# The last stretch of a seven-product block multiplication, in three parts of 256, 128 and 128 tokens in place of two of 256

## Chip, cores and metric

The kernel runs on one core of a Trainium2 chip. Its time is the device time of one execution in microseconds (us). A core has five engines that work beside each other, each through a queue of its own: TensorE (PE in the profile, its weight loads PEld), VectorE (DVE), ScalarE (ACT), GpSimd (POOL) and SyncE (SP), which issues DMAs; ScalarE and GpSimd issue some DMAs too. Engines wait for one another through semaphores.

## What is computed

A trunk of two layers over 1024 tokens of 1024 channels, each a token mixer and a SwiGLU feed-forward part, with RMS norms and scale and gate values made from a conditioning vector, and one RMS norm at the end. Cut to what matters here:

```python
def rms_norm(x, g):
    y = x * rsqrt(mean(x * x, axis=-1, keepdims=True) + EPS)
    return y * g

def swiglu_ffn(h, w_gate, w_up, w_down):
    return (silu(h @ w_gate) * (h @ w_up)) @ w_down

for i in range(DEPTH):
    ...
    h = modulate(rms_norm(x, norm_ffn_g[i]), sh_f, sc_f)
    y = swiglu_ffn(h, ffn_w_gate[i], ffn_w_up[i], ffn_w_down[i])
    x = x + (1.0 + g_f) * y
return rms_norm(x, final_g)
```

The change is in the last product with `w_down` of the second layer and in the final norm of half of the tokens.

## The kernel before

Channels lie on the 128 partitions, so `x` is eight tiles of 128 channels by tokens (k = 0 to 7), and tokens are in two chunks of 512, A (0) and B (1). The tiles of a chunk lie in pairs in SBUF, and two tiles of a pair go out in one DMA.

A weight or an activation is kept as two parts of rounded 32-bit numbers (`F32R`): `hi`, rounded, and `lo`, the rest. A product of the two is three matmuls into one bank of PSUM (`products`, L496): high by high, high by low, low by high. Each matmul loads 128x128 weights and streams the tokens past them. Sums for the norms and the spreading of a row over partitions are matmuls of plain 32-bit numbers, which the trace shows as two records each.

The product with `w_down` in the second layer is done by Strassen's scheme, with seven block products in place of eight (`Seven`, L1489), each over up to six groups of feature blocks (q) and with sums of 512 tokens in four PSUM banks `dn`, one for each output tile. When a product is complete, `update` (L1008) adds it, times the gate, to `x`. The last of the seven, `p3`, is split: its first three groups of q run as the others do and are added to the lower four tiles of chunk B, and the remaining ones (`LAST`, three groups) run in `ending` (L1570). That is the last stretch of the kernel.

In `ending`, `emit` (L1614) goes over the parts of `ENDS` (L37): first tokens 0 to 255 of chunk B, then 256 to 511. For each part and each of the four output tiles d there are 18 matmuls (three groups of two feature blocks, three matmuls each), then on VectorE `x += gate * dn` (a SCALAR_TENSOR_TENSOR `x<-dn,gains,x`), on ScalarE the square (`t<-x`), and on VectorE its sum into `acc`. The squares of the upper four tiles were summed ahead (`upper`, L1602). In the last part the squares of the last two d are not summed on VectorE, but go to the norm's matmuls directly (`STRAIGHT`).

The norm of a part is a generator, `normed` (L1579), that is advanced step by step:

1. It is made behind the part's last d and waits.
2. `var`: one matmul for every 128 tokens and every term of the sum, with the squares as weights and a column of ones as the moving operand, which leaves the mean squares as columns; then the reciprocal root, eight small VectorE instructions on `var` and `col`. ScalarE then multiplies the part of all eight tiles by the final gain (`x<-x,vecs`), at a lower priority.
3. `rstd`: one matmul for every 128 tokens spreads the root over the partitions; ScalarE copies it to SBUF (`ny`); in all parts but the last GpSimd multiplies six of the eight tiles by `ny`.
4. VectorE multiplies the others by `rstd`. In the last part VectorE has six tiles and GpSimd two. Behind each pair of tiles the output's DMA is issued: by ScalarE for k = 1 and 5, by SyncE for k = 3 and 7 (`scaled`, L1572).

While the second part's products run, the first part's norm is advanced at d = 1 (step 2) and d = 3 (step 3). The rest is issued behind the last product. Chunk A's final norm (`final`, L1644) runs in the same stretch, its `rstd` between the products of the first part, and its scalings on VectorE and GpSimd.

TensorE's order is the order in which the code issues it. The other engines' orders are made by a scheduler from the program's order, priorities and its own estimates. Each engine then runs its queue strictly in that order: a DMA that ScalarE issues stands in ScalarE's queue, and what is behind it waits until its data is ready.

Of the kernel before, what the change touches and what calls it, by code (L numbers as in the profile page):

```python
# [33 lines left out]
CHUNKS = ((0, 512), (512, 512))  # L34
CENTRED = (0, 2, 3, 1, 5, 6, 4, 7)

ENDS = ((0, 256), (256, 256))  # L37
NP = NF // 2
GROUP = 4
ROUND = 4  # L40
# [91 lines left out]
def trunk(ctx, tc, xT, c, vec, ada, adan, w1f, w1, wdg, w2, wgu, wdn, wds, wpl, out):  # L132
# [91 lines left out]
    def pace(ahead=AHEAD):  # L224

        for t in [t for t in tasks if t.urgent or getattr(t, "free", False)]:
            while step(t, "V"):
                pass
        moved = True
        while moved and tasks:  # L230
            moved = False
            for e in "VG":
                if clock[e] < clock["PE"] + ahead:
                    moved = any(step(t, e) for t in list(tasks)) or moved
# [62 lines left out]
    def bank(name):  # L297
        return ps.tile([P, 512], F32, tag="mm", name=nm(name))
# [15 lines left out]
    def temp(n, name="t", bufs=0):  # L314
        t = tmp.tile([P, TMPW], F32, tag=name if bufs else "t", name=nm(name), bufs=bufs or 4)
        return t[:, :n]
# [53 lines left out]
    def V(name, j, n=1):  # L370
        b = _COLS[name] + j
        return vecs[:, b : b + n]
# [123 lines left out]
    def products(out, wt, k, act, first, last, o=0, n=None, more=False):  # L496

        wk = slice(k * P, (k + 1) * P)
        for i, (wp, a) in enumerate(((0, 0), (0, 1), (1, 0))):
            cols = act[a][:, o : o + n] if n else act[a]  # L500
            matmul(out, wt[:, wp, wk], cols, start=first and i == 0, stop=last and i == 2, more=more)
# [114 lines left out]
    def xsub(ch, k, o, n):  # L616
        return x[ch.i][k][:, o : o + n]
# [5 lines left out]
    def now(gen):  # L623

        while True:
            try:
                next(gen)
            except StopIteration as e:
                return e.value
# [940 lines left out]
    def ending(ch, l):  # L1570

        def scaled(k, o, n, rstd, eng):  # L1572
            xs = xsub(ch, k, o, n)
            eng.tensor_tensor(xs, xs, rstd, op=MUL)
            if k % 2:
                (nc.scalar if k % 4 == 1 else nc.sync).dma_start(
                    out[:, k - 1 : k + 1, ch.t0 + o : ch.t0 + o + n], xp[ch.i][k // 2][:, :, o : o + n])

        def normed(o, n, acc, last):  # L1579
            steps = mean_rsqrt(acc, n)  # L1580
            next(steps)
            yield
            next(steps)
            with tc.high_priority(offset=-LATER):
                for k in range(KT):
                    S_.activation(xsub(ch, k, o, n), xsub(ch, k, o, n), AF.Copy, scale=V("final_g", k))
            yield
            r = now(steps)
            held = temp(n, "ny", 2)
            S_.copy(held, r)  # L1590
            on_pool = [k for k in range(KT) if (k % 4 == 3 if last else k % 4 != 1)]
            if not last:
                for k in on_pool:
                    scaled(k, o, n, held, G_)
                yield
            for k in range(KT):
                if k not in on_pool:
                    scaled(k, o, n, r, V_)
                elif last:
                    scaled(k, o, n, held, G_)  # L1600

        def upper(take):  # L1602

            for d in range(KT // 2, KT):
                sq = temp(ch.n) if d > KT // 2 else temp(ch.n, "acc", 2)
                S_.activation(sq, x[ch.i][d], AF.Square)
                if d == KT // 2:
                    st["upper"] = sq
                elif d < KT - 1:
                    V_.tensor_tensor(st["upper"], st["upper"], sq, op=ADD)  # L1610
                else:
                    V_.scalar_tensor_tensor(st["upper"], sq, EPS_SUM, st["upper"], op0=ADD, op1=ADD)

        def emit(parts):  # L1614
            behind_it = iter(())
            for s, (o, n) in enumerate(ENDS):
                last, straight = s == len(ENDS) - 1, []
                acc = st["upper"][:, o : o + n]
                for d in range(KT // 2):
                    b = bank("dn")  # L1620
                    todo = [(wt, 4 * i + d, g) for wt, ops in parts for i, g in enumerate(ops)]
                    for j, (wt, k, g) in enumerate(todo):
                        products(b[:, :n], wt, k, g, j == 0, j == len(todo) - 1, o, n)
                    xs = xsub(ch, d, o, n)
                    V_.scalar_tensor_tensor(xs, b[:, :n], gate_f[:, l * KT + d : l * KT + d + 1], xs, op0=MUL, op1=ADD)
                    sq = temp(n)
                    S_.activation(sq, xs, AF.Square)
                    if last and d > STRAIGHT:
                        straight.append(sq)
                    else:  # L1630
                        V_.tensor_tensor(acc, acc, sq, op=ADD)
                    if d in (1, 3):
                        next(behind_it, None)
                    pace()
                earlier, behind_it = behind_it, normed(o, n, [acc, *straight], last)
                next(behind_it)
            next(behind_it)
            for _ in earlier:
                pass
            for _ in behind_it:  # L1640
                pass
        return upper, emit

    def final(ch):  # L1644
# [41 lines left out]
    for k in range(KT):  # L1686
# [4 lines left out]
        if k > 1:  # L1691
            acc = squares[0]
# [344 lines left out]
```

## Time and profile before

| | us |
|---|---|
| the three runs | 1696.59, 1699.11, 3929.37 |
| median | 1699.11 |
| the profiled execution, its own time | 1702.04 |
| its span, from the first to the last instruction | 1700.3 |
| mean granted TensorE clock in it | 0.996 |
| start of the first part's products in the last stretch | 1669.2 |
| end of the last product | 1687.8 |
| last VectorE instruction's end | 1695.6 |

The span lies inside the execution, 1.7 us shorter than its time. In the rows, `out<-in` names tiles without their buffers' numbers, and L148 and L126 are the helpers that issue matmuls and the other engines' instructions, so that one reads by names. PE and PEld overlap: a weight load runs while the matmul before it streams. The duration of one matmul is longer than the distance to the next, since they are pipelined; the price of a matmul in a stream is the distance between two starts.

### The profile page before, as it was taken

The numbers are of one execution on the slowest core, as the hardware profiler recorded it, in microseconds if no ns is written. First come the engines' busy times: TensorE is split into PE (matmuls) and PEld (weight loads), VectorE is DVE, ScalarE is ACT, GpSimd is POOL, SyncE is SP. The second block draws the span as 40 slices with busy tenths as digits, with TensorE's granted clock in tenths as the row PEclk, the third lists the DMA queues.
The fourth block names the chain that finished last, engine by engine and source line by source line (L and its number), as shares of the span: only waits on it lengthen the run. The fifth ranks groups of instructions, "written<-read, shape, count | busy, mean of one in ns | idle before, by whom it ended". The sixth has DMA issues, their size and how long they took to land.

```text
span 1700.3 us, 21323 instructions
## 1 busy us (share of the span) xinstructions
PE 1670.4 (98%) x7614; PEld 1361.6 (80%) x7614; DVE 1319.5 (78%) x1872; ACT 800.3 (47%) x1085; POOL 481.9 (28%) x566
## 2 busy tenths in 40 slices
PE   7999999999999999999999999999999999999997
PEld 5777777778887888888888888888888888888787
DVE  8889899899758887887666897847877767668576
ACT  3669686867546332333223336646422222234363
POOL 3587767796001111221110211100111111000103
PEclk9999999999999999999999999999999999999998
DMA  8958997828685788886877846877677776586832
GB/s 294 294 173 218 234 237 203 223 76 237 213 241 153 256 258 300 281 263 209 340 271 270 260 160 196 231 242 211 183 225 228 212 231 186 195 280 200 237 137 100
DMA packets 115821, 380.71 MB, mean 224 GB/s; under 512 B 12225, under 2 KB 14401, under 8 KB 115714
## 3 DMA queue, kind: packets, MB, share of 16 engines
q1 hardware_dynamic: 77888, 247.46, 41.2%
q0 software_dynamic: 36736, 130.83, 31.3%
q8 instruction: 60, 0.98, 0.2%
q10 hardware_dynamic: 1090, 1.05, 0.2%
q14 instruction: 47, 0.39, 0.1%
HBM read 311.92 MB, written 63.18 MB: 221 GB/s over the span
## 4 chain that ended last, share of the span: by engine, by line
PE 88%; DVE 5%; DMA 3%; issue 1%; POOL 1%; ACT 1%; SPq 0%; DVEq 0%; ACTq 0%
PE a L148 24%; PE dn L148 23%; PE e L148 13%; PE p L148 12%; PE y L148 6%; PE g L148 3%; PE first L148 3%; PE tap L148 2%; DMA raw<-in_wds_dram 1%; POOL pa L126 1%; PE ada L148 1%; DMA adaw<-in_adan_dram 1%; DVE t L126 1%; PE rstd L148 1%; PE var L148 1%
## 5 line engine op out<-in xcount | busy, mean ns | idle before, releaser
L126 ACT CAST w<-raw 128x1024 fp32r<-128x1024 f32 (+1 forms) x249 | 258.9, 1041 | 367.2 <-PE dn L148 105.8
L148 PE MATMUL dn<-g,w 128*128 128x512 f32 x1152 | 265.1, 390 | 2.4 <-DVE x L126 1.0
L126 DVE TENSOR_TENSOR w<-raw,w 128x1024 fp32r<-128x1024 f32 (+1 forms) x177 | 217.9, 1234 | 50.4 <-ACT w L126 49.9
L148 PEld LDWEIGHTS dn<-g,w 128*128 128x128 f32 x1152 | 215.6, 188 | 48.4 <-DVE x L126 1.4
L148 PE MATMUL a<-n,w 128*128 128x512 f32 x1056 | 247.6, 390 | 1.1 <-DVE n L126 0.7
L148 PE MATMUL p<-h,w 128*128 128x512 f32 x1056 | 244.2, 391 | 0.8 <-DVE h L126 0.6
L126 POOL TENSOR_TENSOR pa<-pa,pr 128x512 f32<-128x512 f32 x160 | 227.8, 1503 | 25.4 <-ACT pr L126 19.2
L148 PEld LDWEIGHTS a<-n,w 128*128 128x128 f32 x1056 | 197.8, 188 | 44.1 <-DVE n L126 2.2
L148 PEld LDWEIGHTS p<-h,w 128*128 128x128 f32 x1056 | 197.2, 188 | 43.9 <-DVE h L126 1.5
L148 PE MATMUL dn<-hi,w 128*128 128x512 f32 (+1 forms) x600 | 174.0, 373 | 1.5 <-DVE x L126 1.5
L126 DVE SCALAR_TENSOR_TENSOR ca<-u,vecs,ca 128x512 f32<-128x512 f32 x245 | 169.9, 748 | 0.5
L126 DVE SCALAR_TENSOR_TENSOR x<-dn,gains,x 128x512 f32<-128x512 f32 (+1 forms) x144 | 100.7, 732 | 39.9 <-PE dn L148 39.8
L148 PEld LDWEIGHTS dn<-hi,w 128*128 128x128 f32 x600 | 109.7, 188 | 22.4 <-ACT hi L126 1.5
L148 PE MATMUL a<-t,w 128*128 128x512 f32 x528 | 123.6, 389 | 0.7 <-DVE w L126 0.7
L148 PE MATMUL e<-b,w 128*128 128x512 f32 x528 | 123.4, 389 | 0.6 <-DVE r L126 0.6
L148 PE MATMUL e<-t,w 128*128 128x512 f32 x528 | 123.2, 389 | 0.0
L126 ACT ACTIVATE pr<-u,vecs 128x512 f32<-128x512 f32 x160 | 108.2, 715 | 25.0 <-POOL pa L126 17.3
L148 PEld LDWEIGHTS a<-t,w 128*128 128x128 f32 x528 | 99.0, 188 | 21.7 <-DVE w L126 1.1
L148 PEld LDWEIGHTS e<-b,w 128*128 128x128 f32 x528 | 99.0, 188 | 21.6 <-DVE r L126 1.0
L148 PEld LDWEIGHTS e<-t,w 128*128 128x128 f32 x528 | 99.1, 188 | 20.6
L1108 POOL DMA_DIRECT2D raw<-in_wgu_dram x41 | 36.2, 884 | 277.8 <-DMA raw<-in_wgu_dram 83.0
L148 PE MATMUL dn<-lo,w 128*128 128x512 f32 (+1 forms) x300 | 111.6, 372 | 0.0
(181 smaller groups left out, 2379.6 us busy)
## 6 DMA issues: line engine op xcount, KB each, us to landing
raw<-in_wgu_dram SPq DMA_DIRECT2D x132, 512.0 KB, 4.8
adaw<-in_ada_dram POOLq DMA_DIRECT2D x48, 512.0 KB, 7.0
raw<-in_wdn_dram SPq DMA_DIRECT2D x44, 512.0 KB, 8.2
raw<-in_wgu_dram POOLq DMA_DIRECT2D x41, 512.0 KB, 7.2
raw<-in_w_dram SPq DMA_DIRECT2D x36, 512.0 KB, 6.2
gd<-g POOLq DMA_DIRECT2D x36, 512.0 KB, 7.8
g<-gd SPq DMA_DIRECT2D x36, 512.0 KB, 5.4
kinds<-k POOLq DMA_DIRECT2D x33, 512.0 KB, 6.9
```

The lines of the kernel that those rows point to most:

```text
L126: self.last = self.order(getattr(self.eng, name)(out, *args, **kw))
L148: last_mm[0] = nc.tensor.matmul(out, lhsT, rhs, start=start, stop=stop, skip_group_check=more).ins.name
L1108: d = order(nc.gpsimd.dma_start(w[i], wgu[l, fp, src], accum_op=ADD))
```

## The change

The table of parts gets a third entry, and `emit` keeps all norms in a list rather than the last two by name:

```diff
-ENDS = ((0, 256), (256, 256))
+ENDS = ((0, 256), (256, 128), (384, 128))
...
         def emit(parts):
-            behind_it = iter(())
+            norms = []
             for s, (o, n) in enumerate(ENDS):
...
                     if d in (1, 3):
-                        next(behind_it, None)
+                        for each in norms:
+                            next(each, None)
                     pace()
-                earlier, behind_it = behind_it, normed(o, n, [acc, *straight], last)
-                next(behind_it)
-            next(behind_it)
-            for _ in earlier:
-                pass
-            for _ in behind_it:
-                pass
+                norms.append(normed(o, n, [acc, *straight], last))
+                next(norms[-1])
+            next(norms[-1])
+            for each in norms:
+                for _ in each:
+                    pass
```

The first part stays as it is. Tokens 256 to 511 are now two parts with 72 products of 128 tokens each, and each with its own squares, sums, `var`, root, `rstd`, copy, scalings and four output DMAs of half the size. The norms of both earlier parts are advanced at d = 1 and 3: the first part's steps 2 and 3 fall into the second part, its step 4 and the second part's steps 2 and 3 into the third.

On TensorE, behind the last product of the second part, the first part's `rstd` (13614 before, 13616 now) and what follows it. The names are those of tiles with their running numbers, `hi` and `lo` are activations, `w` weights, `ident` the identity; the last number is the width that is streamed. Before:

```order
L148 MATMUL dn_13592<-lo_13390,w_13386 128x256
L148 MATMUL dn_13592<-hi_13389,w_13386 128x256
L148 MATMUL rstd_13614<-ident,col_13553 128x128 x2
L148 MATMUL var_13627<-ones,acc_13045 128x1
L148 MATMUL var_13627<-ones,t_13590 128x1
L148 MATMUL var_13627<-ones,t_13612 128x1
L148 MATMUL var_13627<-ones,acc_13045 128x1
L148 MATMUL var_13627<-ones,t_13590 128x1
L148 MATMUL var_13627<-ones,t_13612 128x1
L148 MATMUL rstd_13655<-ident,col_13634 128x128 x2
```

And now, at the end of the second part:

```order
L148 MATMUL dn_13593<-lo_13390,w_13386 128x128
L148 MATMUL dn_13593<-hi_13389,w_13386 128x128
L148 MATMUL rstd_13616<-ident,col_13553 128x128 x2
L148 MATMUL dn_13629<-hi_13313,w_13310 128x128
L148 MATMUL dn_13629<-lo_13314,w_13310 128x128
```

and at the end of the third:

```order
L148 MATMUL dn_13720<-lo_13390,w_13386 128x128
L148 MATMUL dn_13720<-hi_13389,w_13386 128x128
L148 MATMUL rstd_13742<-ident,col_13681 128x128
L148 MATMUL var_13754<-ones,acc_13045 128x1
L148 MATMUL var_13754<-ones,t_13718 128x1
L148 MATMUL var_13754<-ones,t_13740 128x1
L148 MATMUL rstd_13779<-ident,col_13758 128x128
```

The first part's `rstd` now stands ahead of the third part's products, and behind the last product there are one, three and one small matmuls where there were two, six and two.

On ScalarE, from the copy of the first part's `rstd` to the end. `t` are squares, `x<-x,vecs` the scalings by the final gain, and the rows of L1576 issue output DMAs, which wait for VectorE's and GpSimd's scalings. Before:

```order
L126 COPY ny_13617<-rstd_13614 128x256
L126 ACTIVATE t_13612<-x_12279 128x256
L126 ACTIVATE x_12279<-x_12279,vecs 128x256
L1576 DMA out_dram<-x_12242 128x2x256
L1576 DMA out_dram<-x_12317 128x2x256
L126 COPY ny_13658<-rstd_13655 128x256
```

And now, up to the second group's square of the third part:

```order
L126 ACTIVATE t_13613<-x_12279 128x128
L126 COPY ny_13619<-rstd_13616 128x256
L126 ACTIVATE x_12279<-x_12279,vecs 128x128
L1576 DMA out_dram<-x_12242 128x2x256
L126 ACTIVATE t_13649<-x_12242 128x128
L126 ACTIVATE x_12242<-x_12242,vecs 128x128
L1576 DMA out_dram<-x_12317 128x2x256
L126 ACTIVATE t_13672<-x_12242 128x128
L126 ACTIVATE x_12242<-x_12242,vecs 128x128
```

The first part's two DMAs on ScalarE, which were issued behind all squares, now stand between squares of the third part.

## Prediction

> **What bounds the kernel now.** First the page's lines on span and engines:
>
> ```profile
> span 1700.3 us, 21323 instructions
> PE 1670.4 (98%) x7614; PEld 1361.6 (80%) x7614; DVE 1319.5 (78%) x1872; ACT 800.3 (47%) x1085; POOL 481.9 (28%) x566
> ```
>
> TensorE (PE) is busy for 98% of the span, so what is added to its stream in the last stretch is added to the time unless something after it gets shorter. Second, the chain of work that ended last, from 1660 us to the end; its columns are start, duration, and what ran, with a count where pieces were merged:
>
> ```profile
> 1659.98 5.67 PE dn L148 x25
> ...
> 1666.43 7.14 PE dn L148 x48
> 1673.57 0.89 PE rstd L148 x8
> 1674.46 8.63 PE dn L148 x72
> 1683.10 0.34 PE var L148 x4
> 1683.43 4.41 PE dn L148 x36
> 1687.84 0.46 PE rstd L148 x4
> ...
> 1688.32 0.37 ACT ny L126
> 1688.69 0.33 ACT t L126
> ...
> 1689.06 1.07 PE var L148 x8
> ...
> 1690.15 0.17 DVE col L126
> ...
> 1691.54 0.17 DVE col L126
> ...
> 1691.85 1.20 PE rstd L148 x4
> ...
> 1693.08 0.38 ACT ny L126
> ...
> 1693.48 0.42 DVE x L126
> ...
> 1694.23 1.32 DVE x L126 x4
> ```
>
> Up to 1687.84 the chain is TensorE without a gap: the two halves of 256 tokens (72 products each, so 144), with eight matmuls for chunk A's final norm and four for the first half's inside. From 1687.84, which I call T, it is a relay from engine to engine: 12.46 us from T to the span's end at 1700.30. So the change has a price before T, in how long the products take, and a gain behind T, in how long the relay is.
>
> **The price of a product of 128 tokens.** This decides the sum, and no row shows it: no `dn` product of before is narrower than 256. The wide ones first. 25 products of 512 tokens in 5.67 us are 0.227 us each; 72 of 256 tokens in 8.63 us are 0.1199. The difference of 0.107 for 256 tokens is 0.42 ns a token, which put on to 128 gives 0.1199 - 0.0534 = 0.0665 us. That is the lower end: only the streaming of tokens is counted. But every product also loads 128 columns of weights. For matmuls that stream one token there is the timeline of the weight loads, and beside it the groups of loads by shape (mean ns after the comma):
>
> ```profile
> 1682.82 0.53 PEld L148 LDWEIGHTS var<-ones,acc 128*128 128x128 f32 x4
> 1687.56 0.53 PEld L148 LDWEIGHTS rstd<-ident,col 128*128 128x128 f32 x4
> ...
> L148 PEld LDWEIGHTS var<-ones,acc 128*128 128x128 f32 x96 | 13.2, 202 | 9.0 <-DVE acc L126 7.6 <-issue 0.4 <-DVE ca L126 0.4
> L148 PEld LDWEIGHTS ada<-adaw,ccols 128*32 128x32 f32 x256 | 5.0, 108 | 12.4 <-issue 10.6 <-DMA adaw<-in_adan_dram 1.8
> L148 PEld LDWEIGHTS dn<-hi,w 128*128 128x128 f32 x600 | 109.7, 188 | 22.4 <-ACT hi L126 1.5 <-DVE x L126 0.8 <-DVE w L126 0.3
> ```
>
> Four loads for one-token matmuls take 0.53 us, and the last of them about 0.19 (188 ns), so they start (0.53 - 0.19)/3 = 0.113 us apart, although there is next to nothing to stream. The loads of `rstd` start the same 0.113 apart. The last two rows tell the same in another way: 32 columns take 108 ns, 128 columns 188 for `dn`, so a column costs 80/96 = 0.83 ns and 128 of them 107 ns. I read 0.113 as the pace of weight loads, which hide behind 256 tokens (0.1199) and stick out behind 128 (0.0665). The upper end is the 512-token product, 0.227: a narrower one of the same kind should not cost more. I take 0.113, since its rows load the same 128x128 shape at the same 188 to 202 ns. The `dn` operands are rounded 32-bit ones and those of `var` plain, so this is an estimate.
>
> The Trainium skill has a rule here that speaks for a cheaper change. TensorE: Matmul & The Clock Gate, section "Back-to-back issue gap", gives about 81 ns a matmul for a stream of load and matmul pairs at 128 tokens. By that the products would cost 144 x 0.081 = 11.7 us and the whole change, an estimate, about +1 us. No run here shows 81 ns, and the two rows of 0.113 stand against it for 32-bit weights.
>
> **Part by part, before T.** (1) The second half's 72 products go, the two quarters' 144 come: 144 x 0.113 - 8.63 = +7.6 us. (2) The first part's two `rstd` products (four records, 0.46 in the chain) stood behind the last product; now a third part follows them, so they lie before T: +0.45. (3) The second part's root needs one `var` product (two records) before T: 2 x 0.113 = +0.23. The four `var` records of the first part stay. T moves by +8.3 us.
>
> Does anything else hold TensorE up? The first part's `var` reads `acc` as VectorE (DVE) leaves it, and VectorE is late there; in the timeline (start, duration, engine, line, operation, out<-in, widths, and the idle time before it):
>
> ```profile
> 1675.12 4.09 DVE L126 TENSOR_TENSOR x<-x,ny 128x512 f32<-128x512 f32 x3
> 1679.14 0.47 DVE L126 SCALAR_TENSOR_TENSOR x<-dn,gains,x 128x256 f32<-128x256 f32 x1
> ...
> 1681.54 0.56 DVE L126 TENSOR_TENSOR acc<-acc,t 128x256 f32<-128x256 f32 x1 [0.48 <-ACT t L126]
> ```
>
> The first half's sums end at 1682.10. Its last product ends near 1674.46 + 8.63/2 = 1678.78; two groups of 18 narrow products later `var` stands at 1678.78 + 36 x 0.113 = 1682.85. That leaves 0.75 us: nothing waits. In the third part ScalarE (ACT) issues the first part's second output DMA ahead of the second group's square, and so stands until the fourth of GpSimd's (POOL) products is done. From
>
> ```profile
> 1688.77 4.14 POOL L126 TENSOR_TENSOR x<-x,ny 128x256 f32<-128x256 f32 x6 [5.53 <-ACT ny L126]
> ...
> L126 POOL TENSOR_TENSOR x<-x,ny 128x512 f32<-128x512 f32 x5 | 8.1, 1644 | 69.3 <-ACT ny L126 69.3
> ```
>
> four take 4 x 0.69 = 2.8 us, starting about 1.1 us after the second part's last product (0.93 in the trace of before, and now a square stands ahead of the copy that starts them): free again at +3.9, while the square is wanted at 0.45 + 36 x 0.113 = +4.5. It hides, with 0.6 us left; queued behind that DMA are only squares and scalings. The 16 scalings by the final gain become 24, the extra ones 8 x 0.3 = 2.4 us of ScalarE at most by the 0.3 that two narrow ones cost over a wide one:
>
> ```profile
> L126 ACT ACTIVATE x<-x,vecs 128x512 f32<-128x512 f32 x8 | 5.0, 714 | 0.0
> L126 ACT ACTIVATE x<-x,vecs 128x256 f32<-128x256 f32 x16 | 7.6, 504 | 0.3
> L126 ACT CAST hi<-op 128x1024 fp32r<-128x1024 f32 x12 | 12.6, 1049 | 14.6 <-PE dn L148 14.5
> ```
>
> (714 and 504 give 0.82 ns a token, so 399 ns for 128.) ScalarE idles 14.6 us ahead of the casts, waiting for TensorE, which covers them. Were that cover gone, 2.4 us would be the most they cost.
>
> **Part by part, behind T.** Widths cost, by the groups of these instructions in the last 100 us:
>
> ```profile
> L126 DVE SCALAR_TENSOR_TENSOR x<-dn,gains,x 128x512 f32<-128x512 f32 x12 | 8.6, 747 | 1.8 <-PE dn L148 1.8
> L126 DVE SCALAR_TENSOR_TENSOR x<-dn,gains,x 128x256 f32<-128x256 f32 x8 | 3.8, 478 | 3.4 <-PE dn L148 3.4
> L126 ACT ACTIVATE t<-x 128x512 f32<-128x512 f32 x10 | 5.8, 621 | 2.2 <-DVE x L126 2.1
> L126 ACT ACTIVATE t<-x 128x256 f32<-128x256 f32 x8 | 3.3, 418 | 12.2 <-DVE x L126 12.2
> ```
>
> - `rstd`, `ny` and the last square `t`: two `rstd` records fewer (-0.23) and a copy and a square 128 tokens narrower at 203/256 = 0.79 ns a token (-0.10 each): -0.43. VectorE's last `x` is then ready in time, 0.34 us after T by 269/256 = 1.05 ns a token.
> - `var`: the last square is awaited by two records in place of eight: -6 x 0.113 = -0.68.
> - The root, eight VectorE instructions on two columns, now on one, is all fixed cost: 0. The second part's two VectorE scalings end about 1.0 us after T, the root starts at 1.15: no wait.
> - The last `rstd`: two records in place of four. They ran at half the clock, as the windows show (length, busy time of PE, PEld, DVE, ACT, POOL, then the granted clock):
>
> ```profile
> 1687.84:1690.90 3.06, 1.84 (x16) 1.67 (x15) 1.88 (x7) 1.20 (x3) 2.13 (x4) 0.99 0.14 48
> 1690.90:1693.10 2.20, 1.19 (x4) 0.93 (x4) 0.67 (x5) 0.03 (x1) 2.01 (x3) 0.50 0.75 256
> ...
> 1693.48 2.08 DVE L126 TENSOR_TENSOR x<-x,rstd 128x256 f32<-128x256 f32 x6 [1.78 <-ACT ny L126]
> ...
> out_dram<-x SPq DMA_DIRECT2D x4, 512.0 KB, 2.8
> out_dram<-x SPq DMA_DIRECT2D x4, 256.0 KB, 2.2
> ```
>
>   1.19 us for four leaves about 0.2 us a record: -0.4.
> - The second `ny`: -0.1. Six VectorE scalings in 2.08 us: 128 tokens fewer at 1.05 ns are 0.13 each: -0.8.
> - The last stores land 0.6 us sooner for 256 KB than for 512; half of that for the next halving: -0.3, between 0 and -0.6.
>
> GpSimd's and SyncE's extra pieces of the second part (six scalings, two DMAs) stand ahead of the last part's: even at the price of 256 tokens, 6 x 0.69 = 4.1 us from 0.55 after T, they end at 4.7. The last part's two are wanted from 4.0 (1.15, 1.6 for the root, 0.1, 0.8 for `rstd`, 0.3 for `ny`), so the bounds are 0 and +0.7; at half that price they end at 2.6, and I take 0.
>
> Together -2.7. **The sum: +8.3 - 2.7 = +5.6 us.** The profiled execution took 1702.04 us, 2.9 above the median of the three runs (1699.11); I add to the median: 1704.7, rounded 1705.
>
> **The rivals.** (A) Streaming bounds, not loading: successive loads overlap more than the `var` rows show, and a product costs 0.0665. Then (1) is 144 x 0.0665 - 8.63 = +0.95, (2) and (3) about +0.4 at that price, and with -2.7 the kernel gets faster: -1.3, 1698. It ends on this side of zero below about (8.63 + 2.3)/144 = 0.076 us a product. For it: a load lasts 188 ns and yet they start 113 apart, so they overlap already; against it: one-token matmuls would show any closer pace. The skill's 81 ns, in the section named above, lies between this rival and mine. (B) A narrow product of rounded operands runs as the plain 32-bit ones do, two records each: 2 x 0.113 = 0.226, the upper end. Then (1) is +23.9 and the time 1721. For it: no narrow one is on record; against it: at 256 and 512 tokens the price is one straight line. Even that is +1.3%. (C) The queue crossing: ScalarE's wait for GpSimd outlasts its 0.6 us of slack. The late square's sum stands on VectorE among the root's instructions of the second part, so that root is late too, and TensorE waits for it ahead of the second `rstd` once the root's own slack, some 2 us, is gone. At the price of GpSimd's 512-token group, 1.64 us, four would end 3.2 us late: 1.2 us more on T, 1706, and 1708 if the root has no slack. Against it: those products are 256 wide, at 0.69.
>
> **How the numbers follow.** Forecast (a product at 0.113 to 0.120, which adds up to 1.0 us): 0.78; A, with all prices below 0.09: 0.11; B: 0.06; C: 0.05. The range: runs of before spread from 1696.59 to 1702.04, so 3 us either way around 1705 and A's 1698 below, C and the 0.120 above: 1698 to 1710, which leaves out B and the lower part of A. A measurement of this kernel can tell about 2% from no change, 34 us; that would need 0.31 us a product, (34 + 2.0 + 8.63)/144, above every bound here. So within 2%: 0.97, slower 0.02, faster 0.01.
>
> **What would show it.** Right: weight loads of the 128-token `dn` products start 0.11 to 0.12 us apart and 36 of them take 4.0 to 4.3 us in the chain; T lies about 8 us later than 1687.84; the stretch from T to the end is 9.3 to 10.3 us, with two `var` records behind the last square and the six scalings in 1.2 to 1.4 us. Wrong: products 0.07 or 0.22 apart, a gap on TensorE ahead of a `var` or `rstd`, or ScalarE's second output DMA ending after the second group's products.

## The result, and the profile after

| | before | after |
|---|---|---|
| runs | 11 | 11 |
| median, us | 1699.92 | 1704.53 |
| lowest and highest, us | 1696.59, 3929.37 | 1701.64, 1709.10 |
| the profiled execution: time, span, us | 1702.04, 1700.3 | 1709.10, 1707.3 |
| ratio after to before, with its 95% interval | | 1.0031 [1.0022, 1.0039] |

The changed kernel is slower by 0.31%, which on 1699.92 us is 5.3 us (3.7 to 6.6): within 2%, and still a difference, since the interval leaves out 1. One of the eleven runs of before took 3929.37 us, for which no trace has a reason; the ratio leaves it out. The page of the kernel after has these lines on the span and the engines:

```profile
span 1707.3 us, 21505 instructions
PE 1678.7 (98%) x7682; PEld 1370.0 (80%) x7682; DVE 1322.4 (77%) x1890; ACT 802.9 (47%) x1098; POOL 484.1 (28%) x572
```

TensorE is busy 8.3 us longer than before, and still for 98% of the span. The chain of work that ended last tells where; start, duration, what ran:

```profile
1668.98 7.14 PE dn L148 x48
1676.12 0.89 PE rstd L148 x8
1677.01 8.29 PE dn L148 x72
1685.30 0.39 PE var L148 x4
1685.69 4.08 PE dn L148 x36
1689.77 0.49 PE rstd L148 x4
1690.26 3.97 PE dn L148 x36
1694.23 0.17 PE var L148 x2
1694.40 4.08 PE dn L148 x36
1698.47 0.29 PE rstd L148 x2
...
1698.78 0.27 ACT ny L126
...
1699.31 0.40 PE var L148 x2
...
1699.73 0.17 DVE col L126
...
1701.42 0.78 PE rstd L148 x2
...
1702.22 0.27 ACT ny L126
...
1702.52 0.29 DVE x L126
...
1703.00 0.79 DVE x L126 x4
```

Two points cut this chain into a stretch and a tail that can be compared between executions. S is the start of the piece with 48 `dn` products: 1666.43 before, 1668.98 after. T is the end of the last `dn` product: 1687.84 and 1698.47. The stretch from S to T was 21.41 us and is 29.49 (+8.08). The tail from T to the span's end was 1700.3 - 1687.84 = 12.46 and is 1707.3 - 1698.47 = 8.83 (-3.63). A span is given to 0.1 us, so two tails compare to about 0.1. The sum is +4.45 us, inside the interval of the ratio. The rest of the 7.0 us between the two spans lies ahead of S, where S itself is 2.55 us later. Nothing is changed there, and runs of one kernel differ by more than that (1701.64 to 1709.10). So stretch and tail are what I compare from here on, and the medians where a kernel ran often.

In the stretch, 36 products of 128 tokens take 4.08, 3.97 and 4.08 us. The piece of 72 holds 36 of 256 and 36 of 128 tokens. In the timeline of the weight loads (start, duration; some rows hold two loads) the price is the distance between starts:

```profile
1690.10 0.19 PEld L148 LDWEIGHTS dn<-lo,w 128*128 128x128 f32 x1
1690.21 0.30 PEld L148 LDWEIGHTS dn<-hi,w 128*128 128x128 f32 x2
...
1691.44 0.19 PEld L148 LDWEIGHTS dn<-lo,w 128*128 128x128 f32 x1
```

From 1690.10 to 1691.44 there are twelve distances of 0.112 us. A load still lasts 0.19 us, so each begins while the one before it runs.

In the tail, the stores are where more was gained than expected. The windows show it (length, busy time of PE, PEld, DVE, ACT, POOL, then granted clock, share of the DMA engines, GB/s). Before:

```profile
1695.00:1696.00 1.00, 0.00 (x0) 0.00 (x0) 0.56 (x2) 0.00 (x0) 0.00 (x0) 0.50 0.82 278
1696.00:1697.00 1.00, 0.00 (x0) 0.00 (x0) 0.00 (x0) 0.00 (x0) 0.00 (x0) 0.50 1.03 340
1697.00:1698.00 1.00, 0.00 (x0) 0.00 (x0) 0.00 (x0) 0.00 (x0) 0.00 (x0) 0.50 1.01 343
```

After, with the last `rstd` in the first row:

```profile
1701.42:1702.20 0.78, 0.76 (x2) 0.47 (x2) 0.00 (x0) 0.00 (x0) 0.22 (x1) 0.50 0.98 288
...
1704.00:1705.00 1.00, 0.00 (x0) 0.00 (x0) 0.00 (x0) 0.00 (x0) 0.00 (x0) 0.50 1.00 286
1705.00:1706.00 1.00, 0.00 (x0) 0.00 (x0) 0.00 (x0) 0.00 (x0) 0.00 (x0) 0.50 0.75 231
```

Before, VectorE is done at 1695.56 and the DMA engines are then full for two more microseconds. So the last store may not only take its own time to land, but stand behind the others, which experiments 4 and 5 try. After, they are full for one and three quarters, and from VectorE's end to the span's end it is 1707.3 - 1703.79 = 3.51 us in place of 1700.3 - 1695.56 = 4.74: 1.23 less.

Last, the crossing on ScalarE that was rival C (timeline of the kernel after):

```profile
1693.67 0.38 ACTq L1576 DMA_DIRECT2D out_dram<-x  x1
1694.65 0.31 ACT L126 ACTIVATE t<-x 128x128 f32<-128x128 f32 x1 [1.26 <-DVE x L126]
```

The second DMA of the first part is off the queue at 1694.05, and the square behind it starts at 1694.65, released by VectorE and not by the queue. The crossing hid, with 0.6 us left.

### The profile page after: what moved, and what is told of

It is laid out like the page before. It is cut to its first block, busy times and chain, and to the rows that moved or that the text cites. A ratio compares the mean times of both kernels' runs of the same rounds, so it can differ in the third digit from the quotient of the medians.

```text
span 1707.3 us, 21505 instructions
## 1 busy us (share of the span) xinstructions
PE 1678.7 (98%) x7682; PEld 1370.0 (80%) x7682; DVE 1322.4 (77%) x1890; ACT 802.9 (47%) x1098; POOL 484.1 (28%) x572
## 4 chain that ended last, share of the span: by engine, by line
PE 90%; DVE 5%; DMA 2%; POOL 1%; issue 1%; ACT 1%; SPq 0%; DVEq 0%; ACTq 0%
PE dn L148 25%; PE a L148 23%; PE e L148 13%; PE p L148 12%; PE y L148 6%; PE g L148 3%; PE first L148 3%; PE tap L148 2%; PE ada L148 1%; POOL pa L126 1%; DMA adaw<-in_adan_dram 1%; DVE t L126 1%; PE var L148 1%; PE rstd L148 1%; DVE ca L126 0%
## 5 line engine op out<-in xcount | busy, mean ns | idle before, releaser
L148 PE MATMUL dn<-hi,w 128*128 128x512 f32 (+2 forms) x648 | 181.7, 365 | 1.6 <-DVE x L126 1.6
L148 PEld LDWEIGHTS dn<-hi,w 128*128 128x128 f32 x648 | 117.0, 189 | 22.3 <-ACT hi L126 1.6
L126 DVE SCALAR_TENSOR_TENSOR x<-dn,gains,x 128x512 f32<-128x512 f32 (+2 forms) x148 | 101.6, 718 | 42.9 <-PE dn L148 42.9
L148 PE MATMUL dn<-lo,w 128*128 128x512 f32 (+2 forms) x324 | 118.1, 364 | 0.0
```

The source lines that it names most:

```text
L126: self.last = self.order(getattr(self.eng, name)(out, *args, **kw))
L148: last_mm[0] = nc.tensor.matmul(out, lhsT, rhs, start=start, stop=stop, skip_group_check=more).ins.name
```

## The experiments

Two things were open. The first is what sets 0.112 us: the loading of 128 columns (theory), or something else of a narrow product, such as its streaming or its issue (rival). The second is what shortened the tail by 0.9 us more than the working had, and whether the gain can be had without the price. Stretch and tail of all kernels, each from its profiled execution:

| kernel | S to T | T to the end | sum |
|---|---|---|---|
| before | 21.41 | 12.46 | 33.87 |
| after | 29.49 | 8.83 | 38.32 |
| 1 more tokens streamed | 30.13 | 8.54 | 38.67 |
| 2 fewer weight columns | 25.97 | 8.97 | 34.94 |
| 3 three product parts, norm of two | 28.83 | 11.88 | 40.71 |
| 4 first part not stored | 21.41 | 11.82 | 33.23 |
| 5 only the last store of the last part | 21.41 | 10.90 | 32.31 |
| 6 parts of 384 and 128 | 24.90 | 12.14 | 37.04 |
| 7 halves, first `rstd` earlier | 21.84 | 11.99 | 33.83 |
| 8 only the last tile in quarters | 24.33 | 9.57 | 33.90 |
| 9 the same, two changes behind it | 24.31 | 9.91 | 34.22 |

**1. More tokens past the same weights.** From the kernel after: the second part's products stream 192 tokens and the third's 256, and only the last 128 of the results are used.

```diff
+                    wide = (0, 64, 128)[s]
...
-                        products(b[:, :n], wt, k, g, j == 0, j == len(todo) - 1, o, n)
+                        products(b[:, : n + wide], wt, k, g, j == 0, j == len(todo) - 1, o - wide, n + wide)
```

> As the changed kernel, but the products of the second part stream 192 tokens and those of the third 256, of which the last 128 are used. I read the stretch from the end of chunk A's var (start of the 48 products in the chain) to the end of the last product, 29.5 us in the changed kernel, and 36 products of a part in the chain, 4.08. Theory (the 128 columns of weights take 0.112 us to load, whatever is streamed below that): 192 tokens would stream in 0.0935 us, so the second part stays at 4.0 to 4.1 us for 36; 256 tokens stream in 0.120, so the third part is 4.3 for 36 and the stretch 30.0 to 30.1. Rival (a narrow product has a fixed floor to which each token adds 0.42 ns): 64 and 128 tokens more add 1.9 and 3.8 us, the stretch is 35.2.

The stretch took 30.13 us. Its chain:

```profile
1680.84 4.11 PE dn L148 x36
...
1685.41 4.31 PE dn L148 x36
...
1689.84 4.42 PE dn L148 x36
```

The first row is half of the second part, with 192 tokens, the others are the third part's halves, with 256. In the kernel after, with 128, the same rows are 4.08, 3.97 and 4.08. Half as many tokens again cost 0.03 us in 36 products, twice as many 0.34. So at 128 the tokens do not set the price, and the stretch is the 30.0 to 30.1 of the theory and not the 35.2 of the rival. (One run took 1704.53 us; eight of the kernel before, median 1698.37.)

**2. Fewer weight columns.** From the kernel after: four of the six feature blocks of each sum in the second part load 96 of the 128 columns, in the third part 64. The other columns of these blocks are left out of the sum.

```diff
+            c = P if first or last else cols_of
+            matmul(out[:c], wt[:, wp, k * P : k * P + c], cols, start=first and i == 0, stop=last and i == 2, more=more)
```

> As the changed kernel, but in four of the six feature blocks of each output tile the products load fewer columns of weights, 96 in the second part and 64 in the third (the other output channels of those products are left out). Theory (loading binds): 96 columns take 96 x 0.833 + 5 = 85 ns, 64 take 58, less than the 67 that 128 tokens stream; of 72 products 48 are narrower, so the second part takes 24 x 0.112 + 48 x 0.085 = 6.8 us in place of 8.06, the third 24 x 0.112 + 48 x 0.067 = 5.9, and the stretch of 29.5 us becomes 26.0. Rival (a floor for a product of 128 tokens that has nothing to do with the columns loaded): 29.5.

The stretch took 25.97 us, 3.52 less than the kernel after, although TensorE lost some 0.2 in it to a wait for `acc` ahead of the first part's `var`. The loads, 96 columns first and 64 below (start, duration):

```profile
1680.32 0.17 PEld L148 LDWEIGHTS dn<-lo,w 128*96 128x96 f32 x1
...
1681.08 0.17 PEld L148 LDWEIGHTS dn<-lo,w 128*96 128x96 f32 x1
...
1685.51 0.14 PEld L148 LDWEIGHTS dn<-lo,w 128*64 128x64 f32 x1
...
1686.05 0.14 PEld L148 LDWEIGHTS dn<-lo,w 128*64 128x64 f32 x1
```

Nine distances in 0.76 us are 0.084 each, nine in 0.54 are 0.060; 128 columns had 0.112. That is 0.8 ns a column, and the products stream 128 tokens in all three. So the price of a narrow product is that of its columns: the theory stands, and the rival falls. (The number of columns is also the number of rows of the result, which this run does not keep apart. For the loading speaks that the loads themselves get shorter, 0.19, 0.17 and 0.14 us, and that the loads of `var`, with one token to stream, kept the same pace.) That the stretch met the expected 26.0 is in part luck: 64 columns were put at 0.067 us, held by the tokens, and took 0.060, which is 0.3 us less for 48 products, and the wait for `acc` made up most of it. (One run, 1700.47 us.)

With cheaper products there is also less time for the other engines, and rival C comes true here. T is 1689.73, and TensorE starts the second part's `rstd` 0.23 us later. The chain, followed back from there, goes through the root, with a late sum inside it, to a DMA on ScalarE that waits for GpSimd:

```profile
1684.57 0.75 POOL x L126
...
1685.34 0.41 ACTq L1577
...
1687.57 0.71 DVE acc L126
...
1689.96 0.47 PE rstd L148 x2
```

**3. Three product parts, but one norm for the last two.** From the kernel after: the products stay in parts of 256, 128 and 128, tokens 256 to 511 get one norm at the end, and all squares are summed on VectorE.

```diff
-                    if last and d > STRAIGHT:
+                    if False:
...
-                    if d in (1, 3):
+                    if s == 2 and d in (1, 3):
...
-                norms.append(normed(o, n, [acc, *straight], last))
+                if s == 1:
+                    continue
+                if last:
+                    o, n = ENDS[1][0], 256
+                norms.append(normed(o, n, [st["upper"][:, o : o + n]], last))
```

> The products of the last stretch in three parts as in the changed kernel, but one norm for tokens 256 to 511 together, behind the last product; its last squares are summed on VectorE. Theory (the products cost, the narrower last norm gives back): stretch to the last product 21.4 + 7.4 = 28.8 us, tail from there to the span's end 12.0 to 12.4 (before 12.46, changed 8.83): var behind the last square 4 records in place of 8, -0.45, the last x and square narrower, -0.25, one sum more, +0.35. In all 7.0 to 7.3 us over before, a ratio of 1.0042. Rival (the tail is shorter because the last products are narrower, not the norm): tail 9 to 9.5, in all +4 to +4.5.

It took 1704.63 us against 1698.37, a ratio of 1.0038 [1.0023, 1.0052]. The stretch is 28.83, the tail 11.88, a little under the expected 12.0 to 12.4 and far from the rival's 9 to 9.5. The price of the products is there in full and most of the gain is gone. So the change is two things that pull against each other, a price of 8.1 us and a gain of 3.6, and the tail is shorter by the norm of 128 tokens, not by the narrower products.

**4. The kernel before without the first part's four stores.** The first 256 tokens of chunk B are not written. The theory was that the stores of both parts queue for the DMA engines at the end, so that taking the first part's away lets the last one land sooner.

```diff
-            if k % 2:
+            if k % 2 and o:
```

> As the kernel before, but the four output stores of the first part (tokens 0 to 255 of chunk B) are left out. In the tail of before the last store is issued at 1695.62 and its landing is seen at 1698.94, 3.3 us later; in the changed kernel 2.4. Theory (the stores of both halves, 2 MB in some 5 us, queue up, and the last lands late): without the first four the last one lands 2.2 to 2.6 us after its issue and the tail of 12.46 us is 11.3 to 11.8. Rival (a store of 256 KB takes that long by its size): 3.2 to 3.4 and 12.3 to 12.5.

The tail fell only to 11.82. From issue to landing the last store took 3.16 us, and 3.32 in the kernel before (1695.62 to 1698.94, where SyncE's wait for it ends). Of the 0.64 that the tail is shorter, 0.16 is this, 0.24 the last `rstd`, which took 0.96 in place of 1.20 (its granted clock was 0.64, and 0.50 before), and some 0.29 the time from the landing to the end (1.07, and 1.36). So this theory fell, and the time to land is close to the rival's 3.2 to 3.4. But the four landings of the last part came at 1693.85, 1694.63, 1695.39 and 1696.13, one each 0.75 us, and that led to the next kernel. (One run, 1699.06 us.)

**5. The kernel before with only the last store of its last part.** Three of the last part's four stores are left out.

```diff
-            if k % 2:
+            if k % 2 and (not o or k == KT - 1):
```

> As the kernel before, but of the last part's four output stores only the last one is issued. Without the first part's stores the last one still landed 3.16 us after its issue, and the four landings were 0.75 us apart. Theory (the last part's own four stores, 256 KB each, drain one behind another at 0.75 us each; in the changed kernel 128 KB each at 0.44): alone it lands 2.1 to 2.5 us after its issue. Rival (a store of 256 KB takes that long by itself): 3.1 to 3.3.

The last store now landed 2.15 us after its issue, 1.17 sooner than in the kernel before, and the tail is 10.90. The windows while it lands:

```profile
1693.00:1694.00 1.00, 0.00 (x0) 0.00 (x0) 0.00 (x0) 0.00 (x0) 0.00 (x0) 0.50 0.30 105
1694.00:1695.00 1.00, 0.00 (x0) 0.00 (x0) 0.00 (x0) 0.00 (x0) 0.00 (x0) 0.50 0.46 157
```

The DMA engines are a third to a half busy where they were full. So the last part's own four stores drain one behind another, and the rival, a store that takes 3.2 us by its size, falls. (One run, 1697.80 us.) In the kernel after they are half as large and land at 1704.94, 1705.38, 1705.82 and 1706.25, 0.44 us apart. The first of the four lands 1.91 us after its issue, the issues take 0.83 us from first to last and the landings 1.31, so the last one lands 1.91 + 1.31 - 0.83 = 2.39 us after its issue. In the kernel before the same sum is 2.17 + 2.50 - 1.35 = 3.32 (issues from 1694.27 to 1695.62, landings from 1696.44 to 1698.94). Of the difference of 0.93 us, 0.26 is the smaller store itself and 0.67 the shorter queue. That is most of the 1.23 us that were gained behind VectorE's end, of which the working had 0.3.

**6. Two parts, of 384 and 128 tokens.** From the kernel before.

```diff
-ENDS = ((0, 256), (256, 256))
+ENDS = ((0, 384), (384, 128))
```

> The last stretch in two parts of 384 and 128 tokens (products of the kernel before otherwise). Theory (a product costs the larger of 0.112 us for its load and 13 ns + 0.417 ns a token; the tail is the relay of the last part and GpSimd's queue): 384 tokens cost 0.173, so 72 x (0.173 + 0.112) = 20.5 us of products against 17.3, and two var records more, +0.2: stretch 21.4 + 3.5 = 24.9. Behind the last product GpSimd has six tiles of 384 tokens, about 1.2 us each between the 0.72 of 256 and the 1.64 of 512, from 1.2 us after it: they end at 8.4, the last part's two at 9.3, the last store lands 2.4 later, in all a tail of 12.3 to 13.2. Sum 3.3 to 4.2 us over before, ratio 1.002. Rival (the tail goes by the width of the last part alone): tail 8.8, sum about 0.

It took 1701.67 us against 1699.26, a ratio of 1.0014 [1.0005, 1.0023]. The stretch of 24.90, as expected, shows a little under half the price, but the tail is 12.14, hardly shorter than with halves and just under the expected 12.3 to 13.2. The rival, a tail of 8.8, falls. GpSimd's timeline says why:

```profile
1690.38 6.58 POOL L126 TENSOR_TENSOR x<-x,ny 128x384 f32<-128x384 f32 x8 [10.45 <-ACT ny L126]
```

It starts 1.3 us after T = 1689.06 with six tiles of 384 tokens, and works without a gap through these and the last part's two until 1696.96. So here the first part's scalings set the end. A middle part takes them off it: with 256, 128 and 128, GpSimd was done with each part before it was wanted.

**7. Halves, with the first part's `rstd` moved ahead.** From the kernel before: the first part's third step is issued early in the last tile, so that only the last part's relay stands behind T. Also `var` runs all tokens of one term before the next term, so that two sums are open in one bank at once, and the last norm has other values. (The Trainium skill, PSUM — Partial Sum Buffer, section "The four PSUM rules", says that a matmul which opens a sum clears the marks of the whole bank, so that the next matmul of another open sum there overwrites what it had. That the values of this run differ fits; its trace cannot show it.)

```diff
-        for i in range(count):
-            for a in parts:
+        for a in parts:
+            for i in range(count):
...
+                        if d == 3 and j == 2:
+                            next(behind_it, None)
...
-                    if d in (1, 3):
+                    if d == 1:
```

> As the kernel before with two halves, but the first half's rstd products and what follows them are issued after half of the last output tile's products, and the norm's var products are ordered by term and not by token block, so that four records and not eight stand behind the last square. Theory: stretch 21.4 + 0.45 = 21.9; behind the last product -0.2 (the square no longer waits for the copy of rstd), -0.45 (var), -0.1 to -0.4 (the first half's stores are done earlier): tail 11.4 to 11.8. Sum 0.2 to 0.6 us under before. Rival (VectorE's scalings of the first half now stand ahead of the last x and hold it up): tail 12.5 or more, sum +0.4 or more.

It took 1699.67 us against 1699.26, a ratio of 1.0004 [0.9995, 1.0013]: no difference. The stretch grew by 0.43, as expected, and the tail fell by 0.47, less than the expected 0.7 to 1.1. Of that, 0.22 is the last `rstd`, which took 0.98 us at a granted clock of 0.63, and 1.20 at 0.50 before. In its chain:

```profile
1684.30 0.42 ACTq L1576
1684.77 0.42 ACT t L126
...
1686.47 0.57 DVE var L126
```

T is 1684.11. The last square stands behind a DMA on ScalarE that waits for GpSimd, which is the crossing of rival C, but at a small cost: VectorE has its input ready at 1684.63, 0.14 us before the square starts. The root starts 0.54 us nearer to T than before (1685.88 - 1684.11 = 1.77, and 2.31). Of that, 0.39 goes again inside the root, where one instruction takes 0.57 in place of 0.18. It ends at 1687.03, just behind a multiplication on GpSimd that ends at 1687.01; in experiment 6 the same instruction takes 0.63 us and ends at 1692.35, GpSimd's at 1692.33. So GpSimd seems to hold it, which no run here was made to test. What could be had from this step alone is no more than what the `rstd` costs ahead of T.

**8. Only the last tile in quarters.** From the kernel before: the second part's first three d run with 256 tokens, only d = 3 runs as two of 128, each with a norm and a relay of its own. By 0.112 a product this costs 36 x 0.112 - 18 x 0.12 = 1.9 us, and not 7.4.

```diff
+            for d in range(3):
+                V_.tensor_tensor(upper_sq[:, 256:], upper_sq[:, 256:], tile_of(d, 256, 256), op=ADD)
...
+            sq = tile_of(3, 256, 128, first)
...
+            second = normed(256, 128, [upper_sq[:, 256:384], sq], False)
+            next(second)
+            sq = tile_of(3, 384, 128, second)
+            third = normed(384, 128, [upper_sq[:, 384:], sq], True)
```

> Tokens 256 to 511 keep products of 256 tokens for three of the four output tiles; only the last tile's products are in two groups of 128 tokens, and each of these 128 tokens has its own norm. The second part's var is issued among the last group's products, its rstd behind them; the first part's rstd among the first narrow group's. Theory (each narrow product costs 0.112, so only the narrow ones pay): 36 x 0.112 - 18 x 0.120 = +1.9, rstd and var ahead of the end +0.9, stretch 24.2; tail as in the changed kernel, 8.5 to 9.2, if the root of the second part is done when the last part's starts. Sum 0.4 to 1.2 us under before and 5 to 6 under the changed kernel. Rival (two norms that end within 2 us of each other stand in each other's way on VectorE and GpSimd): tail 10 to 11, sum +0.3 to +1.3 over before.

It took 1698.87 us against 1699.26, a ratio of 0.9997 [0.9988, 1.0006]. The stretch of 24.33 is as expected, the tail of 9.57 lies between the expected 8.5 to 9.2 and the rival's 10 to 11. The trace shows two waits in it. The last root starts 1.63 us after T = 1690.03, as VectorE's timeline shows:

```profile
1691.66 0.16 DVE L126 TENSOR_SCALAR col<-var 128x1 int32<-128x1 int32 x1 [0.77 <-PE rstd L148]
```

It waits for the `rstd` of the part before, which still reads the one buffer `col`. And the chain runs through GpSimd and ScalarE's queue:

```profile
1692.00 1.71 POOL x L126 x4
...
1694.03 0.42 ACTq L1578
1694.49 0.28 ACT ny L126
```

The last `rstd` is complete at 1694.17, but its copy starts at 1694.49, behind output DMAs of the part before, which wait for GpSimd. That is rival C's mechanism, here at 0.3 us.

**9. The same without these two waits.** `col` gets two buffers, and the second part's DMAs on ScalarE are issued behind the last copy.

```diff
-        cols = tmp.tile([P, 16], F32, tag="col1", name=nm("col"), bufs=1)
+        cols = tmp.tile([P, 16], F32, tag="col1", name=nm("col"), bufs=2)
...
+            if k % 4 == 1 and o == 256:
+                st.setdefault("stores", []).append(store)
...
+                for store in st["stores"]:
+                    tc.add_manual_dep(store().ins, copied, edge, reason="behind the copy")
```

> As last_tile_split, whose tail was 9.57 us, with two waits taken away: the root of the last part waited until the second part's rstd had read the one buffer of col (its first VectorE instruction came 1.63 us after the last product, 1.26 in the changed kernel), so col gets two buffers; and ScalarE's last copy stood behind an output DMA of the second part (0.3 us), so that part's two DMAs are issued behind the copy. Theory: tail 9.57 - 0.37 - 0.3 = 8.9, stretch 24.3 as before it, sum 33.2, 0.6 to 0.7 us under the kernel before, which is too little for its time to show (ratio 0.9996 give or take 0.0009). Rival (GpSimd's six tiles of the second part are what the last two wait for): tail stays at 9.3 or more.

It took 1698.74 us against 1698.86, a ratio of 0.9999 [0.9990, 1.0008]. Both waits are gone: the last root starts 1.30 us after T, and VectorE's last scaling ends 5.41 after T, as in the kernel after (5.32). But the tail is 9.91, longer than in 8 and a full microsecond over the expected 8.9. It is in the rival's range, 9.3 or more, though not for the rival's reason: GpSimd's last scaling ends at 1693.60, ahead of VectorE's. The windows:

```profile
1694.00:1695.00 1.00, 0.00 (x0) 0.00 (x0) 0.00 (x0) 0.00 (x0) 0.00 (x0) 0.50 0.97 276
1695.00:1696.00 1.00, 0.00 (x0) 0.00 (x0) 0.00 (x0) 0.00 (x0) 0.00 (x0) 0.50 0.96 288
1696.00:1697.00 1.00, 0.00 (x0) 0.00 (x0) 0.00 (x0) 0.00 (x0) 0.00 (x0) 0.50 0.52 156
```

VectorE is done at 1693.70, and the DMA engines are full until about 1696.5: the eight stores of 128 KB, of both parts, are now issued within 2.3 us (1691.56 to 1693.89), where the kernel after took 4.2 (1699.61 to 1703.86). From VectorE's end to the span's end it is 4.5 us, where the kernel after has 3.51. By these windows, what was won on the engines was lost in the stores; no run with fewer of them was made here. Beside the same kernel before, 8 and 9 stand at 0.9997 and 0.9999 and the changed kernel at 1.0031: both win back its loss, and neither is faster than the kernel before by anything that can be measured.

## Why the prediction was right

It said 1705.0 us, and the median is 1704.53. That is in part luck, since the changed kernel's profiled execution and its median differ by 4.6 us; the stretch and the tail are the better test. There +5.6 was forecast and +4.45 measured: both terms, +8.3 and -2.7, came out lower, by 0.2 and 0.9 us. The median hides it in part because that of before rose by 0.8 us with more runs (1699.11 to 1699.92).

**Before T** (+8.3 predicted, +8.08 measured). The products: 8.29 + 4.08 + 3.97 + 4.08 - 8.63 - 4.41 = +7.38, where +7.6 was forecast; the price is 0.112 and not 0.113, and the rest of the difference is that the halves had 8.73 us and not 8.63 for their last 72. The first part's `rstd` ahead of T: +0.49 (+0.45). The `var` records: 0.39 + 0.17 - 0.34 = +0.22 (+0.23). The choice of price was the one that decided the forecast, and experiments 1 and 2 show its reason: tokens cost nothing below about 192, columns 0.8 ns each. The reading of it from the `var` loads, matmuls with almost nothing to stream, carried over from plain to rounded operands.

The Trainium skill, TensorE: Matmul & The Clock Gate, section "LDWEIGHTS (loading the stationary operand)", has a load take columns / 1.2 ns, 107 ns for 128. The distances of 112, 84 and 60 ns agree, with some 5 ns on top; the length of a load in the trace, 190 ns for 128 columns, does not. The 81 ns of its section "Back-to-back issue gap" do not appear at 128 columns here.

**No new wait on TensorE**, as argued. The chain shows none ahead of a `var` or `rstd`. The first part's sums end at 1684.61, and `var` starts at 1685.30, 0.69 us later, where 0.75 was worked out (timeline of VectorE after). Both figures are somewhat large, since the loads of these matmuls, which read `acc`, start at 1685.07, only 0.46 us behind it:

```profile
1684.07 0.54 DVE L126 TENSOR_TENSOR acc<-acc,t 128x256 f32<-128x256 f32 x1 [0.48 <-ACT t L126]
...
1702.52 1.28 DVE L126 TENSOR_TENSOR x<-x,rstd 128x128 f32<-128x128 f32 x6 [1.25 <-ACT ny L126]
```

**Behind T** (-2.7 predicted, -3.63 measured), from one row of the chain to the next:

| step | before | after | measured | predicted |
|---|---|---|---|---|
| T to `var`: `rstd`, `ny`, `t` | 1.22 | 0.84 | -0.38 | -0.43 |
| `var` | 1.07 | 0.40 | -0.67 | -0.68 |
| root, from its start to `rstd` | 1.70 | 1.69 | -0.01 | 0 |
| last `rstd` | 1.20 | 0.78 | -0.42 | -0.4 |
| last `ny`, with the gaps beside it | 0.43 | 0.32 | -0.11 | -0.1 |
| six scalings on VectorE | 2.08 | 1.28 | -0.80 | -0.8 |
| VectorE's end to the span's end | 4.74 | 3.51 | -1.23 | -0.3 |

Six of the seven terms are right to 0.05 us. The seventh, "the last stores land 0.6 us sooner for 256 KB than for 512; half of that for the next halving: -0.3, between 0 and -0.6", was mis-sized, and the truth lies outside its bounds. It priced one store by the median from issue to landing, and that hides a queue: by the same view of the kernel after, the gain should even have been 0.1 us,

```profile
out_dram<-x SPq DMA_DIRECT2D x4, 128.0 KB, 2.1
```

against 2.2 for 256 KB. The path, though, ends with the last of four stores, which is the one that waits for the other three (experiments 4 and 5): -0.93, and about -0.3 in the closing waits behind the landing, whose parts I did not separate. So of the signs that were named, the tail missed: 8.83 us, under the 9.3 to 10.3. The others came: loads 0.112 us apart, 36 products in 3.97 to 4.08 (one just under the 4.0), two `var` records behind the last square, six scalings in 1.28. T lies 10.63 us later than 1687.84, of which the stretch is 8.08 and the rest is ahead of S.

**The rivals.** A fell with the price of 0.112; B as well. C hid in the kernel after with the 0.6 us that had been worked out, but it came true in experiment 2, with 0.2 us on TensorE, and its mechanism cost 0.3 us in experiment 8. In both, less time lies between the parts' ends. That GpSimd's and SyncE's extra pieces cost nothing held too. Experiment 6 shows the other side of it, where GpSimd becomes the bound with a first part of 384.

What stays open: why S was 2.55 us later in the profiled execution, and whether a version exists that is faster than the kernel before. The price of quarters can be cut from 8 to 3 us (experiment 8), but the gain is then as small.

## What to carry to other kernels

Before a matmul stream is cut into narrower pieces, compare what one piece streams with what it costs to load its weights: here 128 columns of 32-bit weights cost 0.112 us, so that below about 237 tokens (256 - (0.1199 - 0.112)/0.00042, an estimate, which fits the 0.114 at 192) cutting only adds loads. If a shorter relay behind it is what you want, cutting only the last tile is cheaper (3 us in place of 8); here that just paid for itself, and the queues of the other engines, DMAs included, took part of the gain. And price the end of a kernel by the whole of the bytes that are stored in its last microseconds, not by the landing time of one store.

## What the runs showed of the hardware that was not expected

- The lower bound of the prediction was no bound. 0.0665 us was to be the streaming of 128 tokens, from the line through 256 and 512; with 64 columns a product of 128 tokens took 0.060. So a part of what that line has as fixed is not paid in a stream of narrow products.
- The clock in the tail is not the same from one execution to the next. In the kernel after the last two `rstd` records ran at 0.50 and took 0.78 us (row above). In experiment 1 the same two, as far behind T (2.88 us, and 2.95), ran at full clock in 0.47. Here are that experiment's windows of the root and of `rstd`:

```profile
1695.00:1697.10 2.10, 0.38 (x2) 0.30 (x2) 1.59 (x10) 0.40 (x1) 2.10 (x6) 1.00 0.22 66
1697.14:1697.64 0.50, 0.46 (x2) 0.27 (x2) 0.00 (x0) 0.00 (x0) 0.23 (x1) 1.00 0.98 283
```

  The difference is 0.3 us, so that tails of single executions should not be compared more finely than that. It is the execution and not the kernel: before, experiment 4 and experiment 5 run the same instructions up to the stores, and in narrow windows their granted clock falls from 1.00 to 0.50 about 3.0, 4.3 and 2.7 us after T.
- The last four stores, issued close together, land 0.75 us apart at 256 KB (experiment 4) and 0.44 apart at 128 KB (the kernel after), about 350 and 300 GB/s, close to the rate of the full DMA engines in the windows (340 to 343 and 286 to 288).
- One instruction of the root, `var<-col`, takes 0.17 us, but 0.56 to 0.69 in experiments 2, 6 and 7. In all three it ends 0.02 to 0.03 us behind a multiplication that GpSimd was running when it began. So a relay on VectorE can lose up to 0.5 us to work on GpSimd that it does not wait for in the program; that one holds the other is read from these times alone.
